# Sixteen copies of the bias lines read eight times, the identity's load on another queue, and a third pair of banks in the mixer's projections

## The chip, the cores and the metric

The kernel runs on one core of one Trainium2 chip. The metric is device time in microseconds (us) of one whole execution, the median of several runs. One core has TensorE (PE, matmuls, with its weight loads listed apart as PEld), VectorE (DVE), ScalarE (ACT), GpSimd (POOL) and SyncE (SP), which here only starts transfers; DMA queues move data between the device memory and the core's memory.

## The reference, cut to what matters

Two layers of a decoder trunk on an input of 256 tokens by 1024 channels:

```python
for l in range(2):
    x = x + 0.5 * swiglu(rms_norm(x, norm_gain[l, 0]), w_ffn_in[l, 0], w_ffn_out[l, 0])
    x = x + hybrid_mixer(rms_norm(x, norm_gain[l, 1]), w_in[l], ..., rel_bias)
    x = x + 0.5 * swiglu(rms_norm(x, norm_gain[l, 2]), w_ffn_in[l, 1], w_ffn_out[l, 1])
```

`swiglu` multiplies by a 1024 x 5632 matrix, gates, and multiplies by a 2816 x 1024 matrix. `hybrid_mixer` has one wide input projection (8420 columns) whose columns feed four attention branches (A: top-64 selection, B: one block of 256 keys, C: low-rank latents with rotary keys, D: three dilated windows) and four sigmoid gates; the branches are projected, gated, summed and projected once more. Branches A, B and D add a bias that depends on the distance between query and key, from one table `rel_bias` that both layers share:

```python
bias = bias_table[:, rel_bucket(dist)]          # 20 heads, 32 buckets
logits = einsum(q, k) * scale + bias
```

## The kernel before

Activations stay on the chip. Weights stream once from device memory, 237 MB in all, through five buffers of 1 MB (`raw`), filled in order by the queue of SP; a load waits until its buffer is free. Every product of 32-bit numbers is made from two parts of each factor: `split` (L172) lets ACT cast a weight to its high part `whi` (L187) and DVE (sometimes POOL) subtract to get the low part `wlo` (L188); `mm3` (L191) then runs three matmuls, `mm2` (L196) two with the weights held still. So PE needs three things for a piece of weight: the transfer, the cast, the subtraction.

The program is a chain of six blocks, FFN, mixer and FFN in each layer. `ffn` (L223) loops j from 0 to 10 over 256 columns of the gate and the value half (`up`) and, one step behind, over two rows of 128 of the output matrix (`down`). In the first FFN the loop calls `setup` once, at j = 3 (L356). `setup` (L403) loads the small tables through ACT's queue, and makes the bias: a 21 x 384 table of lines (20 heads and the mask) is built by one matmul, sent to device memory (`ld`, L421), copied there 128 times (`rep`, 4032 KB, L426) and read back skewed by one element per partition, so that partition p holds the distances of query p (`bias`, 2688 KB, L428). The order of DMAs inside `setup` is fixed. All three go through SP's queue, among the weights.

`mixer` (L469) computes ten projections of the normalised input, one after the other: column starts 804, 0, 384, 1316, 1700, 1988, 2500, 3012, 3524 and 4036. Each takes a pair of PSUM banks from `tiles` (L478): banks a2 and a3 in one turn, the double bank a01 in the next. Between them come the uses of a projection: `head_rsqrt` (square on ACT L461, sum on DVE L463, mean L111, power on POOL L114, product L116), the scaled heads `zn` on DVE (L544, L640), and their transposes by matmuls with the identity on PE (L531). The scores of branch B (`sl`, L829, softmax steps L576, L587 and L589) use the banks of a01; the low-rank products (`cqs`, `cks`, L764) and the gates (L884) use the two buffers of the pool pm.

What sets the order: a scheduler simulates the program and orders each engine's instructions by readiness, so that a change of banks or of a DMA's place moves instructions on all engines. Where two strands are joined by hand, the order of PE, ACT and DVE is pinned.

At the start, x is loaded by SP, `ident` (the 128 x 128 identity, L94) by POOL's queue, `rows` (the gains, L100) by ACT's queue; the first PE instruction (L102) transposes `rows` with `ident`, then x is transposed (L132), scaled by DVE (`xg`, L135) and split (`h`, L136 on ACT, L139 on DVE).

Of the kernel before, what the change touches and what calls it, by code (L numbers as in the profile page):

```python
# [9 lines left out]
F32 = mybir.dt.float32  # L10
# [7 lines left out]
T = 256  # L18
NT = 2
# [11 lines left out]
NLINE = 21  # L31
LLEN = 384
# [36 lines left out]
def tile_trunk(ctx: ExitStack, tc: tile.TileContext, a: dict, out: bass.AP):  # L69
    nc = tc.nc  # L70
# [8 lines left out]
    dr = ctx.enter_context(tc.tile_pool(name="dr", bufs=1, space=bass.MemoryType.DRAM))  # L79
    pa = ctx.enter_context(tc.tile_pool(name="pa", bufs=1, space=PSUM))  # L80
    pm = ctx.enter_context(tc.tile_pool(name="pm", bufs=2, space=PSUM))
# [9 lines left out]

    load_x(0)
    ident = const.tile([128, 128], F32, name="ident")
    nc.gpsimd.dma_start(out=ident[:], in_=a["ident"])  # L94

    ones = const.tile([128, 128], F32, name="ones")
    nc.vector.memset(ones[:], 1.0)
# [64 lines left out]
    def raw_tile(name="raw"):  # L162
        return raw_p.tile([128, 2048], F32, name=name, tag="raw")
# [59 lines left out]
    def ffn(l, s, nxt=None, aside=None):  # L223
# [10 lines left out]
        def load_up(j):  # L234
            rv = []
            for g in range(2):
                rv.append(raw_tile()[:].rearrange("p (k n) -> p k n", k=KC))
                c0 = g * DFF + j * 256
                if early:
                    for q in range(2):  # L240
                        nc.sync.dma_start(out=rv[g][:, 4 * q:4 * q + 4], in_=wi[:, 4 * q:4 * q + 4, c0:c0 + 256])
                        if j == g == q == 0:
                            load_x(1)
                else:
                    nc.sync.dma_start(out=rv[g], in_=wi[:, :, c0:c0 + 256])
            return rv
# [10 lines left out]
        def up_first(j, w):  # L257

            for c in range(2):
                act[2 * j + c] = pair_tile()  # L260
            for i in range(NT):
                t = slice(i * 128, (i + 1) * 128)
                ps = pm.tile([128, 2, T], F32, name="pm", tag="pm")
                for g in range(2):
                    for k in range(KC):
                        wh, wl = w[2 * g + k // 4]
                        mm3(ps[:, g, :], hh[:, k, t], hl[:, k, t], wh[:, k % 4, :], wl[:, k % 4, :],
                            k == 0, k == KC - 1)
                    if i == 0:
                        yield  # L270
                sl = wk.tile([128, T], F32, name="sl", tag="sl")
                nc.scalar.activation(out=sl[:], in_=ps[:, 0, :], func=AF.Silu, scale=rs[:, i:i + 1])
                av = wk.tile([128, T], F32, name="av", tag="av")
                nc.vector.scalar_tensor_tensor(out=av[:], in0=ps[:, 1, :], scalar=rs[:, i:i + 1], in1=sl[:],
                                               op0=ALU.mult, op1=ALU.mult)
                if j == i == 0:
                    while todo:
                        todo.pop(0)()
                pst = pt.tile([128, 4, 128], F32, name="pt", tag="pt")
                for c in range(2):  # L280
                    nc.tensor.transpose(pst[:, c, :], av[:, c * 128:(c + 1) * 128], ident[:])
                for c in range(2):
                    ah, al = act[2 * j + c]
                    nc.scalar.copy(ah[:, t], pst[:, c, :])
                    nc.vector.tensor_tensor(al[:, t], pst[:, c, :], f(ah[:, t]), op=ALU.subtract)
# [64 lines left out]
        for j in range(1, NFF // 2):  # L350
            if j < 2:
                for _ in up_first(j, w1):
                    pass
            else:
                up(j, load_up(j))
            if aside and j == 3:  # L356
                aside()
            for m in ((2 * j - 4, 2 * j - 3) if j > 1 else ()):
                w = down_w(m)
                for i in range(NT):  # L360
                    down(m, w, i)
# [36 lines left out]
    bias = const.tile([128, NLINE, T], F32, name="bias")  # L398
# [3 lines left out]

    def setup():  # L403

        oh = wk.tile([32, LLEN], F32, name="oh", tag="xn")
        tc.keep_in_program_order(nc.scalar.dma_start(out=oh[:], in_=a["onehot"]))
        rb = wk.tile([32, 32], F32, name="rb", tag="sl")
        nc.vector.memset(rb[:], 0.0)
        tc.keep_in_program_order(nc.scalar.dma_start(out=rb[0:20, :], in_=a["rel_bias"]))
        dm = wk.tile([NLINE, LLEN], F32, name="dm", tag="e", bufs=3)  # L410
        tc.keep_in_program_order(nc.scalar.dma_start(out=dm[:], in_=a["dmask"]))
        ps = pt.tile([128, 512], F32, name="pt", tag="pt")
        nc.tensor.transpose(ps[:32, :32], rb[:], ident[:32, :32])
        rbt = wk.tile([32, 32], F32, name="rbt", tag="av")
        nc.vector.tensor_copy(rbt[:], ps[:32, :32])
        ps = pt.tile([128, 512], F32, name="pt", tag="pt")
        nc.tensor.matmul(ps[:NLINE, :LLEN], lhsT=rbt[:, :NLINE], rhs=oh[:], start=True, stop=True)
        line = wk.tile([NLINE, LLEN], F32, name="line", tag="e", bufs=3)
        nc.vector.tensor_tensor(line[:], ps[:NLINE, :LLEN], dm[:], op=ALU.add)
        ld = dr.tile([NLINE, LLEN], F32, name="ld")  # L420
        tc.keep_in_program_order(nc.sync.dma_start(out=ld[:], in_=line[:]))  # L421
        rep = dr.tile([NLINE, 128, LLEN], F32, name="rep")
        rv = rep[:]
        lv = ld[:]
        src = bass.AP(tensor=lv.tensor, offset=lv.offset, ap=[[LLEN, NLINE], [0, 128], [1, LLEN]])
        tc.keep_in_program_order(nc.sync.dma_start(out=rep[:], in_=src))  # L426
        src = bass.AP(tensor=rv.tensor, offset=rv.offset + 127, ap=[[LLEN - 1, 128], [128 * LLEN, NLINE], [1, T]])
        tc.keep_in_program_order(nc.sync.dma_start(out=bias[:], in_=src))  # L428

        def load(dst, src):  # L430
            tc.keep_in_program_order(nc.scalar.dma_start(out=dst, in_=src))

        for i in range(NT):
            load(rope[:, i, :], a["rope"][i * 128:(i + 1) * 128, :])
        for qk in range(2):
            for l in range(DEPTH):
                load(gc[:, qk, l, :], a["qk_gain_c"][l, qk:qk + 1, :].partition_broadcast(128))
        gr = wk.tile([96, 128], F32, name="gr", tag="sl")
        nc.vector.memset(gr[64:96, :], 0.0)
        load(gr[0:64, :], a["b_gate"].rearrange("l n (c p) -> (l n c) p", p=128))  # L440
        for j, nm in enumerate(("qk_gain_a", "qk_gain_b", "qk_gain_d")):
            for e in range(2):
                load(gr[64 + 4 * j:68 + 4 * j, 64 * e:64 * e + 64], a[nm].rearrange("l q c -> (l q) c"))
        load(gr[76:82, :], a["mla_norm_q"].rearrange("l (c p) -> (l c) p", p=128))
        load(gr[82:86, :], a["mla_norm_kv"].rearrange("l (c p) -> (l c) p", p=128))
        ps = pt.tile([128, 512], F32, name="pt", tag="pt")
        nc.tensor.transpose(ps[:, :96], gr[:], ident[:96, :96])
        nc.vector.tensor_copy(gT[:], ps[:, :96])
        nc.vector.tensor_scalar(out=gT[:, 0:64], in0=gT[:, 0:64], scalar1=0.5, scalar2=None, op0=ALU.mult)
        for j in range(3):  # L450
            for l in range(DEPTH):
                c = 64 + 4 * j + 2 * l
                nc.vector.tensor_scalar(out=gT[:, c:c + 1], in0=gT[:, c:c + 1], scalar1=0.125, scalar2=None,
                                        op0=ALU.mult)
        nc.vector.tensor_scalar(out=gc[:, 0], in0=gc[:, 0], scalar1=96.0 ** -0.5, scalar2=None, op0=ALU.mult)

    def head_rsqrt(v, nh, w, by=None):

# [10 lines left out]
    def mixer(l, nxt):  # L469
        wi = a["w_in"][l].rearrange("(k p) n -> p k n", p=128)  # L470

        turn = [0]
# [4 lines left out]

        def tiles():  # L478
            turn[0] += 1
            if turn[0] % 2:  # L480
                return [pa.tile([128, 512], F32, name="zp", tag=f"a{2 + i}")[:] for i in range(NT)]
            z = pa.tile([128, 2, 512], F32, name="zp", tag="a01")
            return [z[:, 0, :], z[:, 1, :]]
# [477 lines left out]
        for h in range(2):  # L961
            for q in range(2):
                rv = raw_tile()[:].rearrange("p (k n) -> p k n", k=4)
# [19 lines left out]
    blocks = []  # L983
    for l in reversed(range(DEPTH)):
        blocks.insert(0, ffn(l, 1, (blocks[0], l + 1, 0) if blocks else None))
        blocks.insert(0, mixer(l, (blocks[0], l, 2)))
        blocks.insert(0, ffn(l, 0, (blocks[0], l, 1), None if l else setup))
    main, stats, h = norm(0, 0)
    todo = next(blocks[0])
    main(0)  # L990
# [43 lines left out]
```

## Time and profile before

| what | value |
|---|---|
| median of 3 runs | 1386.67 us (1386.07 to 1387.12) |
| profiled execution | 1388.2 us, of which the profile's span is 1386.4 us |
| PE busy, share of the span | 1351.8 us, 98% |
| DVE, ACT, POOL busy | 951.3, 687.5, 337.3 us |
| HBM read | 234.51 MB, 173 GB/s over the span |
| rep, bias | 4032 KB and 2688 KB |

Busy times of different engines overlap. Idle time of PE is the span less its busy time; the granted clock is the TensorE clock as a share of its full 2.4 GHz. Stretches are given in us from the span's start. The two layers run the same code at different times (the mixer's projections lie at about 230 to 320 us in the first and 915 to 1000 us in the second).

### The profile page before, as it was taken

To read this page: it belongs to the slowest core of one execution; us is meant where nothing else is said; L and a number is where in the kernel's file an instruction comes from. 1 tells how busy PE (TensorE), PEld (TensorE's weight loads), DVE (VectorE), ACT (ScalarE), POOL (GpSimd) and SP (SyncE) were. 2 spreads that over 40 slices of the span, in tenths; PEclk is the share of its full clock that TensorE was granted. 3 is DMA by queue.
4 is the path that set the end of the run, shared out by engine and by line. 5 is a ranking of instruction groups with operands and counts; after the bars stand their busy time and mean duration, and the time that the engine had idled before them with its cause. 6 is when DMAs were issued, how large, how long until landed. Compare 5 with 4: busy or idle time off the path is not lost.

```text
span 1386.4 us, 21269 instructions
## 1 busy us (share of the span) xinstructions
PE 1351.8 (98%) x8241; PEld 1195.4 (86%) x8241; DVE 951.3 (69%) x1642; ACT 687.5 (50%) x1052; POOL 337.3 (24%) x281
## 2 busy tenths in 40 slices
PE   7998999999999999999999999999999999999998
PEld 7887889879988989888898888898789989888887
DVE  6747756777587686666577766567865976776663
ACT  6425444655454556444454444355554455554441
POOL 0212342140022041322502232323300412222231
PEclk9999999999999999999999999999999999999999
DMA  9549733545343365655556555354543424665530
GB/s 356 168 165 371 246 119 118 184 150 185 114 136 117 122 203 193 209 185 183 182 167 198 182 183 197 96 170 155 180 140 122 153 92 136 210 209 196 193 122 31
DMA packets 173589, 236.96 MB, mean 171 GB/s; under 512 B 5085, under 2 KB 144545, under 8 KB 173489
## 3 DMA queue, kind: packets, MB, share of 16 engines
q1 hardware_dynamic: 172275, 235.16, 51.3%
q8 instruction: 65, 1.06, 0.3%
q10 hardware_dynamic: 1182, 0.38, 0.1%
q14 instruction: 35, 0.29, 0.1%
q0 software_dynamic: 32, 0.07, 0.0%
HBM read 234.51 MB, written 5.21 MB: 173 GB/s over the span
## 4 chain that ended last, share of the span: by engine, by line
PE 90%; DVE 5%; ACT 2%; issue 1%; DMA 1%; POOL 1%; SPq 0%; ACTq 0%; DVEq 0%; POOLq 0%
PE pt L199 9%; PE pm L199 9%; PE pm L192 7%; PE pm L194 7%; PE pm L193 7%; PE acc L192 6%; PE acc L193 6%; PE acc L194 6%; PE pt L200 5%; PE pm L200 5%; PE zp L193 4%; PE zp L194 4%; PE zp L192 4%; PE ov L604 2%; DVE wlo L188 2%
## 5 line engine op out<-in xcount | busy, mean ns | idle before, releaser
L187 ACT CAST whi<-raw 128x1024 fp32r<-128x1024 f32 (+5 forms) x446 | 452.3, 1020 | 416.6 <-PE pm L193 96.9
L188 DVE TENSOR_TENSOR wlo<-raw,whi 128x1024 fp32r<-128x1024 f32 (+3 forms) x426 | 514.3, 1212 | 167.7 <-ACT whi L187 165.4
L199 PE MATMUL pt<-h,whi 128*128 128x512 f32 x576 | 210.5, 399 | 2.9 <-ACT whi L187 2.9
L199 PE MATMUL pm<-h,whi 128*128 128x512 f32 x576 | 208.5, 396 | 0.0
L308 POOL TENSOR_TENSOR sl<-sl,rb 128x256 f32<-128x256 f32 x72 | 82.9, 1151 | 326.1 <-ACT sl L307 324.6
L200 PE MATMUL pt<-h,wlo 128*128 128x256 f32 x576 | 150.5, 282 | 0.8 <-DVE wlo L188 0.8
L200 PE MATMUL pm<-h,wlo 128*128 128x256 f32 x576 | 149.6, 280 | 0.0
L192 PE MATMUL pm<-h,whi 128*128 128x256 f32 x512 | 148.0, 289 | 1.3 <-DVE tg L922 1.3
L194 PE MATMUL pm<-h,wlo 128*128 128x256 f32 x512 | 147.1, 287 | 0.0
L193 PE MATMUL pm<-h,whi 128*128 128x256 f32 x512 | 146.8, 287 | 0.0
L193 PE MATMUL acc<-wlo,act 128*128 128x512 f32 x352 | 138.4, 393 | 0.0
L194 PE MATMUL acc<-whi,act 128*128 128x512 f32 x352 | 138.0, 392 | 0.0
L192 PE MATMUL acc<-whi,act 128*128 128x512 f32 x352 | 137.9, 393 | 0.0
L199 PEld LDWEIGHTS pt<-h,whi 128*128 128x128 f32 x576 | 109.0, 189 | 22.9 <-ACT whi L187 3.2
L199 PEld LDWEIGHTS pm<-h,whi 128*128 128x128 f32 x576 | 108.2, 188 | 20.8 <-issue 0.6
L312 POOL TENSOR_TENSOR act<-av,act 128x256 fp32r<-128x256 f32 x72 | 83.4, 1159 | 165.3 <-ACT act L311 157.5
L193 PE MATMUL zp<-wlo,h 128*128 128x512 f32 (+4 forms) x320 | 115.9, 363 | 1.1 <-DVE wlo L188 1.1
L200 PEld LDWEIGHTS pt<-h,wlo 128*128 128x128 f32 x576 | 109.4, 190 | 7.3 <-DVE wlo L188 1.1
L194 PE MATMUL zp<-whi,h 128*128 128x512 f32 (+4 forms) x320 | 114.4, 358 | 0.0
L200 PEld LDWEIGHTS pm<-h,wlo 128*128 128x128 f32 x576 | 108.7, 189 | 6.4
L192 PE MATMUL zp<-whi,h 128*128 128x512 f32 (+4 forms) x320 | 110.1, 361 | 1.2 <-ACT whi L187 1.2
L192 PEld LDWEIGHTS pm<-h,whi 128*128 128x128 f32 x512 | 97.7, 191 | 5.3 <-issue 4.3
(200 smaller groups left out, 2485.6 us busy)
## 6 DMA issues: line engine op xcount, KB each, us to landing
raw<-in_w_ffn_in_dram SPq DMA_DIRECT2D x66, 1024.0 KB
raw<-in_w_in_dram SPq DMA_DIRECT2D x52, 1024.0 KB
raw<-in_w_ffn_out_dram SPq DMA_DIRECT2D x44, 1024.0 KB
raw<-in_w_ffn_in_dram SPq DMA_DIRECT2D x44, 512.0 KB
raw<-in_w_branch_dram SPq DMA_DIRECT2D x8, 1024.0 KB
raw<-in_w_out_dram SPq DMA_DIRECT2D x8, 1024.0 KB
raw<-in_w_in_dram SPq DMA_DIRECT2D x8, 768.0 KB
rep<-ld SPq DMA_DIRECT2D x1, 4032.0 KB
```

The costliest lines, as they stand in the source:

```text
L187: nc.scalar.copy(hv, src)
L188: (eng or nc.vector).tensor_tensor(lv, src, f(hv), op=ALU.subtract)
L192: nc.tensor.matmul(ps, lhsT=lh, rhs=rh, start=start, stop=False)
L193: nc.tensor.matmul(ps, lhsT=lh, rhs=rl, start=False, stop=False)
L194: nc.tensor.matmul(ps, lhsT=ll, rhs=rh, start=False, stop=stop)
L199: parts = [lambda: nc.tensor.matmul(ps, lhsT=wh, rhs=r2, start=start, stop=stop), lambda: nc.tensor.matmul(ps[:, 0], lhsT=wl, rhs=r2[:, 0] ...
L200: lambda: nc.tensor.matmul(ps[:, 0], lhsT=wl, rhs=r2[:, 0], start=False, stop=False)]
L308: nc.gpsimd.tensor_tensor(sl[:], sl[:], rb[:], op=ALU.mult)
L312: nc.gpsimd.tensor_tensor(al, av[:], f(ah), op=ALU.subtract)
L604: nc.tensor.matmul(o[:, h, :], lhsT=pT[:, j, :], rhs=pv(j), start=j == 0, stop=j == nb - 1)
```

## The change

Three edits.

- The bias: `rep` holds 16 copies of the whole table of lines (16 x 8064 elements, 504 KB) instead of 128 copies of each line, and `bias` is filled by eight reads of 16 partitions (336 KB each) instead of one of 128. `setup` is a generator that is advanced once in each step of the FFN's loop: at j = 3 everything but the copies and reads, at j = 4 the copies, at j = 5 to 8 two reads each.
- `ident` is loaded by ACT's queue, ahead of `rows`.
- `tiles` of the mixer takes its banks in three turns: the two buffers of pm, the double bank a01, banks a2 and a3.

```diff
-    nc.gpsimd.dma_start(out=ident[:], in_=a["ident"])
+    nc.scalar.dma_start(out=ident[:], in_=a["ident"])
...
-            if aside and j == 3:
-                aside()
+            if aside and j > 2:
+                next(aside, None)
...
-        rep = dr.tile([NLINE, 128, LLEN], F32, name="rep")
-        rv = rep[:]
-        lv = ld[:]
-        src = bass.AP(tensor=lv.tensor, offset=lv.offset, ap=[[LLEN, NLINE], [0, 128], [1, LLEN]])
-        tc.keep_in_program_order(nc.sync.dma_start(out=rep[:], in_=src))
-        src = bass.AP(tensor=rv.tensor, offset=rv.offset + 127, ap=[[LLEN - 1, 128], [128 * LLEN, NLINE], [1, T]])
-        tc.keep_in_program_order(nc.sync.dma_start(out=bias[:], in_=src))
...
+        yield
+        rep = dr.tile([16, NLINE * LLEN], F32, name="rep")
+        lv, rv = ld[:], rep[:]
+        src = bass.AP(tensor=lv.tensor, offset=lv.offset, ap=[[0, 16], [1, NLINE * LLEN]])
+        tc.keep_in_program_order(nc.sync.dma_start(out=rv, in_=src))
+        for b in range(8):
+            if b % 2 == 0:
+                yield
+            src = bass.AP(tensor=rv.tensor, offset=rv.offset + 127 - 16 * b,
+                          ap=[[NLINE * LLEN - 1, 16], [LLEN, NLINE], [1, T]])
+            tc.keep_in_program_order(nc.sync.dma_start(out=bias[16 * b:16 * b + 16], in_=src))
...
-            if turn[0] % 2:
+            if turn[0] % 3 == 1:
+                return [pm.tile([128, 512], F32, name="zp", tag="pm")[:] for i in range(NT)]
+            if turn[0] % 3 == 0:
                 return [pa.tile([128, 512], F32, name="zp", tag=f"a{2 + i}")[:] for i in range(NT)]
             z = pa.tile([128, 2, 512], F32, name="zp", tag="a01")
             return [z[:, 0, :], z[:, 1, :]]
...
-        blocks.insert(0, ffn(l, 0, (blocks[0], l, 1), None if l else setup))
+        blocks.insert(0, ffn(l, 0, (blocks[0], l, 1), None if l else setup()))
```

Lines behind the edits of `setup` stand about eight lines further down in the changed kernel (L531 is L539 there, L589 is L597, L762 is L770).

SP's queue in the first FFN, where `setup` puts its transfers among the weights (`raw` from L241 are halves of `up` weights, those from L329 `down` weights), as a piece of the difference:

```order
-L421 DMA ld<-line 21x384
-L426 DMA rep<-ld 2688x1x384
+L423 DMA ld<-line 21x384
+L455 DMA rep<-ld 16x8064
 L241 DMA raw<-in_w_ffn_in_dram 128x4x256 x2
-L329 DMA raw<-in_w_ffn_out_dram 128x2x1024
-L241 DMA raw<-in_w_ffn_in_dram 128x4x256 x2
-L428 DMA bias<-rep 128x21x256
-L241 DMA raw<-in_w_ffn_in_dram 128x4x256 x2
+L461 DMA bias<-rep 16x21x256 x4
 L329 DMA raw<-in_w_ffn_out_dram 128x2x1024
```

The copies keep their place behind `ld`; four of the eight reads come directly behind the next two weight loads, the other four further down.

PE in the first mixer, at the end of branch B (`ov` is probabilities times values, `pt<-ident,bo` transposes branch B's output, `pm<-br` multiplies it with its output weights, `pm<-h_1926` or `pm<-h_1933` are the gates). Before:

```order
L194 MATMUL pm<-h_1926,wlo 128x256
L604 MATMUL ov<-bv,pT 128x65 x2
L618 MATMUL pt<-ident,bo 128x128 x2
L597 MATMUL pt<-ident,e 128x128
L604 MATMUL ov<-cv,pT 128x65
```

After, in the same place:

```order
L194 MATMUL pm<-h_1933,wlo 128x256
L626 MATMUL pt<-ident,bo 128x128 x2
L605 MATMUL pt<-ident,e 128x128
L612 MATMUL ov<-cv,pT 128x65
L605 MATMUL pt<-ident,e 128x128
L192 MATMUL pm<-br,whi 128x256 x2
L612 MATMUL ov<-cv,pT 128x65
```

The two products `ov<-bv` (L612) have moved forward: 21 matmuls `pm<-h_1933` now stand between them and the transposes of `bo` (L626).

ACT in the first mixer, during the projection from column 4036, whose weights are cast in pieces of 128 x 512 (`cq`, `ck` are branch C's transposed heads, `e` the exponentials of the scores). Before:

```order
L762 COPY cq<-pt 96x4x128
L187 CAST whi<-raw 128x512
L762 COPY ck<-pt 96x4x128
L187 CAST whi<-raw 128x512
L187 CAST whi<-raw 128x1024 x2
```

After:

```order
L770 COPY cq<-pt 96x4x128
L187 CAST whi<-raw 128x512
L597 ACT_TABLE_LOAD
L597 ACTIVATE e<-e,nm 128x128 x4
L187 CAST whi<-raw 128x512
L770 COPY ck<-pt 96x4x128
L187 CAST whi<-raw 128x512
L187 CAST whi<-raw 128x1024
```

The table load and four exponentials of branch B, which before stand behind all casts of the projections, now stand ahead of the last two casts of 128 x 512; on DVE the softmax steps L576 and L587 move with them.

## Rows read from the trace of the kernel before

**Rows 1.** The page: busy time by engine; the chain that ended last.

```profile
PE 1351.8 (98%) x8241; PEld 1195.4 (86%) x8241; DVE 951.3 (69%) x1642; ACT 687.5 (50%) x1052; POOL 337.3 (24%) x281
PE 90%; DVE 5%; ACT 2%; issue 1%; DMA 1%; POOL 1%; SPq 0%; ACTq 0%; DVEq 0%; POOLq 0%
```

**Rows 2.** PE's waits, by line: line <- releaser: us in total, times, longest.

```profile
PE pt L531 <- DVE zn L544: 3.3, 4, 1.2
PE pt L618 <- DVE bo L611: 2.1, 2, 1.0
PE ov L604 <- DVE pT L601: 1.4, 2, 0.7
PE pt L531 <- DVE zn L640: 1.2, 2, 0.6
```

**Rows 3.** Timeline of SP: start, duration, issue.

```profile
78.54 0.88 SPq L426 DMA_DIRECT2D rep<-ld  x1
79.59 21.38 SPq L241 DMA_DIRECT2D raw<-in_w_ffn_in_dram  x2
106.44 2.38 SPq L428 DMA_DIRECT2D bias<-rep  x1
```

**Rows 4.** Stretches: start:end, length, busy of PE, PEld, DVE, ACT, POOL, clock, DMA share, GB/s.

```profile
80.00:98.00 18.00, 18.00 (x102) 15.59 (x101) 12.05 (x24) 5.31 (x8) 3.58 (x4) 1.00 0.45 163
106.00:112.00 6.00, 2.32 (x12) 1.56 (x11) 1.47 (x2) 2.54 (x3) 0.00 (x0) 1.00 1.02 364
112.00:118.00 6.00, 6.00 (x26) 5.18 (x26) 6.00 (x7) 3.90 (x6) 3.25 (x2) 0.72 1.09 365
```

**Rows 5.** Timelines of ACT and PE at 109 us; idle time before and its releaser in brackets.

```profile
109.46 3.89 ACT L187 CAST whi<-raw 128x1024 fp32r<-128x1024 f32 x4 [14.47 <-DMA raw<-in_w_ffn_in_dram]
110.56 0.50 PE L199 MATMUL pt<-h,whi 128*128 128x512 f32 x1 [2.93 <-ACT whi L187]
```

**Rows 6.** The start: the chain's piece of `ident`; timelines of PE and ACT.

```profile
1.25 4.72 DMA ident<-in_ident_dram
...
6.01 0.34 PE L102 MATMUL pt<-ident,rows 48*128 48x48 f32 x1 [6.01 <-DMA ident<-in_ident_dram]
...
4.38 0.63 ACT L145 ACTIVATE junk<-x 128x512 f32<-128x512 f32 x1 [1.89 <-DMA x<-in_x_dram]
```

**Rows 7.** Timelines of PE at two transposes of the first mixer, and PE's pace.

```profile
237.51 0.41 PE L531 MATMUL pt<-ident,zn 128*128 128x128 f32 x2 [0.62 <-DVE zn L640]
...
237.94 0.34 PE L193 MATMUL zp<-wlo,h 128*128 128x384 f32 x1
238.11 0.34 PE L194 MATMUL zp<-whi,h 128*128 128x384 f32 x1
...
277.56 0.66 PE L531 MATMUL pt<-ident,zn 128*128 128x128 f32 x4 [0.46 <-DVE zn L544]
```

**Rows 8.** Stretches of the first mixer: the low-rank part, the last projections, branch B's end.

```profile
290.00:300.00 10.00, 6.84 (x34) 4.94 (x33) 7.37 (x16) 6.58 (x11) 5.70 (x4) 1.00 0.41 136
300.00:320.00 20.00, 20.00 (x123) 17.75 (x122) 19.38 (x52) 9.86 (x14) 4.67 (x5) 1.00 0.65 206
352.00:356.00 4.00, 2.25 (x15) 1.84 (x15) 3.72 (x11) 2.98 (x7) 0.11 (x1) 0.88 0.23 91
354.00:360.00 6.00, 5.45 (x35) 5.33 (x35) 2.77 (x12) 2.28 (x8) 0.00 (x0) 0.72 0.01 3
```

**Rows 9.** Groups of DVE (busy, mean ns | idle), 250 to 420; timelines of DVE, ACT.

```profile
L587 DVE TENSOR_SCALAR nm<-mx 128x1 f32<-128x1 f32 x20 | 2.0, 146 | 0.0
...
L576 DVE CUSTOM_DVE_ANT_0 e<-sl,bias 128x128 f32<-128x128 f32 x8 | 1.9, 287 | 2.1 <-PE sl L829 1.6 <-PE pt L597 0.5
...
353.08 1.22 DVE L188 TENSOR_TENSOR wlo<-raw,whi 128x1024 fp32r<-128x1024 f32 x1
...
312.94 0.62 ACT L187 CAST whi<-raw 128x512 fp32r<-128x512 f32 x1 [2.21 <-issue]
...
323.65 1.28 ACT L589 ACT_TABLE_LOAD   x1
```

## The prediction

> **What bounds the kernel now.** I read the page first. PE is busy 98% of the span and makes up 90% of the chain that ended last; DVE, the next engine, is busy 69% [rows 1]. PE does the same matmuls after the change, so what can be won is only the time in which it stands still, 1386.4 - 1351.8 = 34.6 us, and the time in which its granted clock is below 1.00. Then I read PE's waits, to see whose they are [rows 2], and the stretches in which PE is not full, to see how long each is and what the clock does behind it [rows 4, 8]. The three edits touch three such places.
>
> The largest is at 106 to 112 us, where PE is busy for 2.32 of 6 us [rows 4]. The matmul at 110.56 had waited 2.93 us for a cast on ACT, and ACT itself had stood idle for 14.47 us until a weight landed [rows 5]. SP tells why: `rep` is issued at 78.54, the next two weight loads hang in the queue from 79.59 for 21.38 us, and only then come the rest [rows 3]. While `rep` runs, 80 to 98, the DMA engines are busy 45% and move 163 GB/s; in 106 to 118 they are full at about 365 GB/s [rows 4]. So for some 20 us the weights stand behind a transfer that uses less than half of the engines. PE lives on what was loaded before: the loads issued before `rep` feed it to 110.56 - 2.93 = 107.6 us [rows 5], 28 us after 79.59.
>
> **The bias: -5.4 us.** What goes if the hole closes is 6 - 2.32 = 3.7 us of waiting, and behind it the clock: 112 to 118 is granted 0.72 on the mean (some of it at the lower level, 1.2 GHz), which costs 6 x 0.28 = 1.7 us [rows 4]. Together 5.4 us. Does it close? The new `rep` is 504 KB, an eighth: at the 163 GB/s of the old one 3.1 us, at 365 GB/s 1.4 us. Behind it two weight loads of 512 KB, then four reads, 1.38 MB, then weights again. The reads have no row here. The nearest ones bound them: 3.8 us at 365 GB/s, 8.4 us at 163 GB/s [rows 4]. So the weights behind them come at most 3.1 + 8.4 + 1.0/0.163 = 17.7 us after 79.6, with ten of the 28 us to spare; this holds over the whole bound, so I take the full 5.4. What is late next is nothing near: ACT and DVE are idle before the hole (ACT 5.31 and DVE 12.05 of 18 us busy in 80 to 98 [rows 4]), and the last four reads, with 0.69 MB each time, stand in front of weights at a time when five buffers are full again. The other steps of `setup` stay where they are.
>
> The rule that speaks against these reads stands in the Trainium skill, "SBUF — State Buffer", section "Door 1: The DMA port swizzle": partitions 0 to 15 are reached by four ports, measured there at 104 GB/s. By it the four reads take an estimated 13 us instead of 3.8 to 8.4 and the hole still closes, with about five us left; no run so far shows such a transfer. The same skill, "DMA: Bandwidth & Descriptors", section "Why a DMA increments its semaphore by 16 and not by 1", lets the slowest dimension set how many engines share a transfer, 7 for one of 21 and 16 for the new one of 16; the 45% busy share during the old `rep` (7 of 16 is 44%) agrees with it.
>
> **The identity: -0.2 us.** PE's first instruction waits 6.01 us for `ident`, whose transfer takes 4.72 us from 1.25; x is there at 4.38 [rows 6]. On ACT's queue the load is issued about 0.5 us sooner and may land with x, so up to 6.0 - 4.5 = 1.5 us could go. But in the changed order DVE makes the first `wlo` (1.22 us, such as the one in [rows 9]) ahead of the scaled x, and ACT takes the second tile's statistics before it casts `h`. What PE wins at the transposes it waits for at the first product of `h`. Bounds: -1.5 (all of it) to +1.2 (the `wlo` on the path); I take -0.2, since the two nearly cancel.
>
> **Three pairs of banks: waits of projections, -2.1 us.** With two pairs in turns, PE cannot begin the next-but-one projection until the uses of this one are over, so the transposes at L531 stand between projections with little work in front. At 237.51 and 277.56 they wait 0.62 and 0.46 us [rows 7]; in both layers that makes the 1.2 of the second L531 row and 0.9 out of the 3.3 of the first [rows 2]. In the changed order of PE there are 23 matmuls of the next projection ahead of them, at 0.17 us each (237.94 to 238.11) some 4 us [rows 7], far over both waits. I take all, 2.1.
>
> **The low-rank part, -0.5 us.** In 290 to 300 PE is idle 3.16 us, POOL's power on eight heads among the causes [rows 8]. In the changed order the same low-rank matmuls stand ahead of the same transposes, so most of it stays: 0 to -1 us per layer, -0.25 each.
>
> **Branch B's end, -0.6 and -1.7 us.** PE waits for `bo` (2.1 us in two waits) and `pT` (1.4 in two) [rows 2]; at 352 to 356 it is busy 2.25 of 4 us and the clock in 354 to 360 is 0.72, another 6 x 0.28 = 1.7 us [rows 8]. The 21 gate matmuls that now stand ahead of L618 take 2.5 us and cover `bo`. But DVE's order now has a `wlo` of 1.22 us [rows 9] ahead of the step that makes `br` for the next products, of which PE's own work there covers some 0.3: about 0.9 us come back, and about 0.5 of the `pT` wait stays. 1.75 becomes 1.4 or 1.5 per layer, -0.3 each, -0.6 in all. Whether the clock falls is open. After 1.75 us of idle time within 4 us it fell; with 3.16 us spread over ten (290 to 300) it stayed at 1.00 [rows 8]. The new waits lie between those two rows, so I take half of the two dips (2 x 1.7), -1.7, and keep 0 and -3.4.
>
> **What moves into the last projections, +1.0 us.** Branch B's scores and softmax steps now lie inside 300 to 320, where DVE is already busy 19.38 of 20 us [rows 8]. DVE gets four L576 of 0.29 us, two of twice the elements, at most 0.57 each, and six L587 of 0.15 [rows 9]: 3.2 us. ACT gets the table load, 1.28, and four exponentials, each at most the 0.62 of a cast with four times the elements [rows 9]: 3.8 us against 2.21 idle just before that cast. On the other side PE gets the score matmuls there too, which gives both engines time. From below the cost is 0 or a gain (the same steps no longer stand behind the projections), from above all 7.0 us per layer. Each excess alone, about 1.5 us on ACT, is met by slack of a like size, so I take 0.5 per layer, 1.0 in all.
>
> **The sum.** -5.4 - 0.2 - 2.1 - 0.5 - 0.6 - 1.7 + 1.0 = -9.5 us. The profiled execution took 1388.2 us with its span of 1386.4, and would take 1378.7; it lies 1.5 us over the median of the runs, 1386.67. For the median: **1377.2 us**.
>
> **The rivals.** (A) Branch B's end is cleared whole: the gate matmuls cover every wait (2.9 us more), the clock never falls there (1.7 more), and nothing stalls in 300 to 320 (1.0). For it: there are 2.5 us of new cover; against it: the `wlo` ahead of `br`. 1371.6 us.
> (B) The hole stays, so that the bias edit does nothing. One engine of the old `rep` moved 163/7 = 23 GB/s (an estimate, if seven of 16 worked, as 45% says). If a read of 16 partitions runs on one or two engines, the four take 30 to 60 us and the weights miss the 28. Against it: the old read of 128 partitions ran in a stretch at 365 GB/s with the weights. 1382.6 us.
> (C) **Slower.** DVE and ACT become the bound at 300 to 320 and 980 to 1000: L587 waits for scores, the exponentials for L587, the cast behind them for the exponentials, its `wlo` for the cast, PE for that. If nothing overlaps it costs 7.0 us a layer, 14 in all in place of the 1.0: 1390.2 us. It decides from 5.3 us of new PE idle time in each layer there (10.5 over two layers eats all gains). For it: 19.38 of 20 us; against it: DVE's list there has steps that nobody waits for soon.
> (D) The identity gives its whole 1.5 us: 1375.9 us.
>
> **How the numbers follow.** Forecast 0.60, A 0.13, B 0.10, C 0.10, D 0.07. What a measurement can tell from no change here is about 0.2%, 2.8 us: below 1383.9 is faster, above 1389.4 slower. Forecast with its bounds, A, D and two thirds of B lie below, with about 0.05 of the forecast's own spread taken off for dips that stay, start at its worst and stalls of a few us: faster 0.82. The rest of B, that 0.05 and a part of C make 0.11 for the same, C's remainder 0.07 for slower. The range goes from 1370.5 (A with a little of the low-rank part) to 1385.0 (B with a slow start), which leaves out most of C and the case that A, D and the low-rank part come together, about 0.18.
>
> **What would show it.** Right: no PE wait for `whi` near 107 us and a clock of 1.00 in 112 to 118; weights issued soon after `rep`, DMA share well over 0.45 there; no waits at L539 after the second and fifth projections; 300 to 320 with PE idle under 1 us. Wrong: a hole that only moved, to where the last four reads stand; PE idle for over 3 us in the last projections; the dip at branch B's end unchanged in both layers, which costs 1.7 of the sum; a first `h` product no earlier, or later, than 10 us.

## The result and the profile after

The changed kernel takes **1378.35 us** (1377.51 to 1378.57, 4 runs), the kernel before 1386.89 us (1386.07 to 1387.39, 4 runs); the ratio is 0.9937 with an interval of 0.9924 to 0.9949. That is 8.5 us faster, where 9.5 were forecast. Some parts of the forecast hit and some missed, and the misses to either side nearly cancel, so part of the closeness is luck.

First the page of the changed kernel, busy time by engine and the chain, as in [rows 1].

```profile
span 1376.7 us, 21253 instructions
PE 1349.9 (98%) x8241; PEld 1193.8 (87%) x8241; DVE 951.8 (69%) x1642; ACT 689.4 (50%) x1052; POOL 334.7 (24%) x280
PE 92%; DVE 4%; ACT 2%; issue 1%; POOL 1%; DMA 0%; SPq 0%; ACTq 0%; DVEq 0%
```

PE's idle time went from 34.6 to 26.8 us, its busy time down by 1.9. Next the stretches that answer to [rows 4, 8]; columns as there.

```profile
88.00:98.00 10.00, 10.00 (x59) 8.73 (x58) 8.48 (x11) 5.30 (x8) 3.18 (x3) 1.00 1.16 117
106.00:112.00 6.00, 6.00 (x36) 5.21 (x35) 5.23 (x7) 3.73 (x6) 2.68 (x2) 1.00 1.17 155
112.00:118.00 6.00, 6.00 (x35) 5.22 (x34) 4.72 (x7) 2.61 (x4) 2.35 (x2) 1.00 1.02 339
290.00:300.00 10.00, 8.83 (x44) 6.88 (x43) 9.18 (x22) 5.74 (x9) 6.14 (x5) 1.00 0.46 148
300.00:320.00 20.00, 20.00 (x129) 17.16 (x129) 17.94 (x59) 12.13 (x21) 1.01 (x1) 1.00 0.50 160
344.00:350.00 6.00, 4.89 (x40) 4.45 (x39) 4.53 (x10) 3.63 (x8) 0.11 (x1) 1.00 0.40 123
350.00:356.00 6.00, 6.00 (x51) 5.56 (x50) 3.89 (x11) 2.22 (x4) 0.00 (x0) 1.00 0.14 57
```

The hole at 106 to 112 is gone, and so is the low clock behind it. The last projections (300 to 320) have no PE idle time. Branch B's end (344 to 350) waits 1.11 us where [rows 8] show 1.75, and the clock behind it stays at 1.00. PE's waits, to hold against [rows 2]:

```profile
PE pt L102 <- DMA rows<-in_norm_gain_dram: 5.8, 1, 5.8
PE pt L539 <- DVE zn L552: 2.4, 2, 1.2
PE ov L612 <- DVE pT L609: 1.3, 2, 0.7
PE ov L612 <- ACT pT L607: 0.9, 2, 0.5
```

The waits for the second `zn` row and for `bo` are no longer there, and of the first `zn` row only the two of the low-rank part are left. The first instruction now waits for `rows`.

A table made from the start times of the same PE instruction in both traces tells where the 9.6 us of the two profiled executions lie. Each row's difference holds all that came before it.

| PE instruction | before, us | after, us | difference |
|---|---|---|---|
| transpose of `rel_bias`, L413 (L415), first FFN | 71.72 | 73.10 | +1.38 |
| first `zp` product of the first mixer | 206.04 | 201.75 | -4.29 |
| first `pt<-ik,aqk`, behind branch B, first mixer | 378.40 | 371.60 | -6.80 |
| first `zp` product of the second mixer | 888.46 | 881.55 | -6.91 |
| first `pt<-ik,aqk` of the second mixer | 1061.03 | 1051.47 | -9.56 |
| last `acc` product | 1382.18 | 1372.62 | -9.56 |

So the start lost 1.4, the hole gave 5.7, each mixer gave 2.5 to 2.65, and all of it by the end of branch B. Two things stick out. The start is longer, not shorter. And the first mixer gave only 2.5 although its waits and low clock, added up (0.62, 0.46, 0.3, 0.64 and 1.7), had gone by 3.7.

### The profile page after: what moved, and what is told of

Same layout as the page of the kernel before. It is cut to its first block, busy times and chain, and to the rows that moved or that the text cites. A ratio compares the mean times of both kernels' runs of the same rounds, so it can differ in the third digit from the quotient of the medians.

```text
span 1376.7 us, 21253 instructions
## 1 busy us (share of the span) xinstructions
PE 1349.9 (98%) x8241; PEld 1193.8 (87%) x8241; DVE 951.8 (69%) x1642; ACT 689.4 (50%) x1052; POOL 334.7 (24%) x280
## 4 chain that ended last, share of the span: by engine, by line
PE 92%; DVE 4%; ACT 2%; issue 1%; POOL 1%; DMA 0%; SPq 0%; ACTq 0%; DVEq 0%
PE pt L199 10%; PE pm L199 10%; PE pm L192 7%; PE pm L194 7%; PE pm L193 7%; PE acc L193 6%; PE acc L192 6%; PE acc L194 6%; PE pt L200 5%; PE pm L200 5%; PE zp L193 4%; PE zp L194 4%; PE zp L192 4%; PE ov L612 2%; DVE wlo L188 1%; PE sl L837 1%
```

## The experiments

Theory after this reading: the three edits act apart, the identity's move costs because it changes an order, and the scores of branch B that moved forward steady the clock but make PE's own steps dearer. The rivals are written in the expectations.

### Each edit alone, and the change without the identity's move

`e1` is the kernel before with only this:

```diff
-    nc.gpsimd.dma_start(out=ident[:], in_=a["ident"])
+    nc.scalar.dma_start(out=ident[:], in_=a["ident"])
```

> The kernel before with only the identity's load on ScalarE's queue, ahead of the gains. Theory (from where the two traces drift apart): the start got 1.4 us longer, because the changed order puts the second tile's statistics, whose x lands at 7.85 us, ahead of the second weight's cast; so 1386.9 + 1.4 = 1388.3 us. Rival (the prediction's term): the earlier issue is worth 0.2 us, up to 1.5; 1386.7 to 1385.4 us, and the 1.4 us of the trace belongs to something else.

`e2` has only the bias edit (`setup` and its calls), `e3` only the three lines of `tiles`.

> The kernel before with only the sixteen copies, the eight reads and their places in the loop. Theory: the hole at 107 us and the low clock behind it go, 5.4 to 5.7 us: 1381.2 to 1381.5 us, PE's order elsewhere as before. Rival: the hole closed only because the changed start delays the demand for weights by 1.4 us; then PE waits for weights again near 107 us, 1383 us or more.

> The kernel before with only the three pairs of banks in the mixer. Theory: each mixer wins 2.5 us (3.75 us of idle and low-clock time less some 1.2 us that the scattered scores add to PE's own steps): 1381.8 us, no drop of the clock at branch B's end in either layer. Rival: the clock holds at branch B's end only because everything before it moved; then the drops of 1.7 us stay in this kernel, 1385 us.

`e4` is the changed kernel with the first diff undone.

> The changed kernel with the identity back on GpSimd's queue. Theory: the three edits add up, and this leaves out the one that costs: 1378.35 - 1.4 = 1377.0 us. Rival: the identity's move wins its 0.2 us and the rest of the kernel pays for something else: 1378.5 us or a little more.

| kernel | median, us | ratio to before (95%) | mean granted clock | mean of span x clock, us |
|---|---|---|---|---|
| before (17 executions beside these) | 1387.36 | 1 | 0.9964 | 1380.7 |
| e1, identity | 1388.68 | 1.0007 (0.9997 to 1.0017) | 0.9966 | 1381.6 |
| e2, bias | 1382.48 | 0.9964 (0.9952 to 0.9976) | 0.9974 | 1376.9 |
| e3, banks | 1381.97 | 0.9962 (0.9949 to 0.9974) | 0.9990 | 1379.0 |
| e4, bias and banks | 1377.24 | 0.9930 (0.9918 to 0.9942) | 0.9998 | 1375.4 |
| after, all three | 1378.35 | 0.9937 (0.9924 to 0.9949) | 1.0000 | 1376.3 |

The medians of e2 and e3 add up: 4.9 + 5.4 = 10.3, and e4 wins 10.1. So e3 and e4 came within 0.3 us of what was expected, and e2 1.0 us above it. The last column, the span times its granted clock, is a measure worked out here for the time without the low clock. It is an estimate: the clock is on record to three decimals, which is 0.7 us of the span of one execution either way, and a low clock costs less than it counts where PE waits. It splits the win of e4: 5.3 us are waits (3.8 of the bias, 1.7 of the banks, which is 5.5) and the rest is clock.

The kernel before draws its clock anew in each execution: of 60 executions beside the experiments 6 had 1.000 with spans of 1382.3 to 1382.9 us, and 8 had 0.995 with 1386.7 to 1387.8. Each drop that comes costs up to 1.7 us, and the same wait may bring it or not. In e2 branch B's end waits 1.75 us in both layers (the last window below begins inside the first of two waits and shows 1.50 of it), with no drop in the first layer and with one in the second:

```profile
106.00:112.00 6.00, 6.00 (x36) 5.21 (x35) 4.12 (x6) 2.98 (x4) 2.20 (x2) 1.00 1.14 117
112.00:118.00 6.00, 6.00 (x33) 5.16 (x32) 5.27 (x8) 2.82 (x4) 2.90 (x3) 1.00 1.03 360
344.00:352.00 8.00, 6.25 (x46) 5.66 (x46) 5.68 (x20) 4.12 (x10) 0.11 (x1) 1.00 0.39 129
1028.00:1036.00 8.00, 6.50 (x44) 6.20 (x44) 4.76 (x15) 4.27 (x11) 0.00 (x0) 0.79 0.04 17
```

The profiled executions give a count. Where branch B's end waits 1.75 us (before, e1, e2 and, below, e5, e6 and e9, two layers each) the clock fell behind it in 6 of 12 places; where it waits 1.1 us or less (after, e3, e4, e7, e8, e10, e11 and e12) in none of 16. So in e3 too it holds with nothing but the banks changed, against the rival of e3. Behind the hole it fell each time that there was one (before, e1, e3 and e7).

The first two lines above also refute the rival of e2: the hole closes without the changed start. By the start times of the same instructions e2 is 0.02 us behind the kernel before until the hole and 5.65 ahead after it.

e1 alone lies inside its interval around no change, so its time does not decide. Its trace does: the first product with `wlo` is 0.75 us later than before, and the same matmul 0.85 later at 24 us and 0.90 at the end. In the column without the low clock it costs 0.9, and so does the step from e4 to after (1375.4 to 1376.3). The start of the changed kernel shows the mechanism, PE, DVE and ACT by start and duration:

```profile
5.84 0.31 PE L102 MATMUL pt<-ident,rows 48*128 48x48 f32 x1 [5.84 <-DMA rows<-in_norm_gain_dram]
8.85 1.97 PE L132 MATMUL pt<-ident,x 128*128 128x128 f32 x8 [0.79 <-DVE xg L135]
10.84 0.58 PE L192 MATMUL pm<-whi,h 128*128 128x256 f32 x1
12.18 0.58 PE L194 MATMUL pm<-whi,h 128*128 128x256 f32 x1 [0.55 <-DVE h L139]
...
6.96 1.23 DVE L188 TENSOR_TENSOR wlo<-raw,whi 128x1024 fp32r<-128x1024 f32 x1 [0.56 <-ACT whi L187]
8.11 1.28 DVE L135 TENSOR_TENSOR xg<-pt,gn 128x512 f32<-128x512 f32 x2
10.29 1.23 DVE L188 TENSOR_TENSOR wlo<-raw,whi 128x1024 fp32r<-128x1024 f32 x1 [0.84 <-ACT whi L187]
11.44 1.29 DVE L139 TENSOR_TENSOR h<-xg,h 128x512 fp32r<-128x512 f32 x2
...
7.87 0.63 ACT L145 ACTIVATE junk<-x 128x512 f32<-128x512 f32 x1 [0.93 <-DMA x<-in_x_dram]
9.22 1.04 ACT L187 CAST whi<-raw 128x1024 fp32r<-128x1024 f32 x1
```

Before, PE transposed both tiles of x without a wait, and the first product started at 9.80:

```profile
6.28 3.87 PE L132 MATMUL pt<-ident,x 128*128 128x128 f32 x16
9.80 0.56 PE L192 MATMUL pm<-whi,h 128*128 128x256 f32 x1
```

With the identity ahead on the same queue, `rows` became the last to land, and PE's first instruction came only 0.17 us sooner (6.01 in [rows 6]). The rest is the changed order. DVE makes the first `wlo` (6.96) ahead of `xg` (8.11), so PE waits 0.79 us for `xg` at the second half of its transposes, and the first product comes at 10.84, straight behind them. On ACT the second tile's statistics stand ahead of the second cast. That tile lands at 7.8 us, ACT stands for it, and the cast comes at 9.22; DVE makes its `wlo` (10.29) ahead of `h` (11.44), for which PE waits 0.55 us at 12.18. e1 shows the same two waits, 0.83 and 0.49 us. PE's products behind them begin 0.21 us apart (12.98, 13.19) where before they begin 0.12 apart (11.11, 11.23); the clock column shows 1.00 for both, so the reason for this pace stays open. The kernel before loses 0.92 us to two later waits that the changed one does not have, and at 24 us the difference is 1.4.

### Is it the transfer or the order?

`e8` issues the identity from SP's queue right behind x, so that VectorE keeps the old order.

```diff
-    nc.scalar.dma_start(out=ident[:], in_=a["ident"])
+    nc.sync.dma_start(out=ident[:], in_=a["ident"])
```

> The changed kernel with the identity issued by the queue of SP, right behind the first tile of x. Theory: what costs at the start is the order on ScalarE and VectorE (the second tile's statistics and the first low part ahead of the scaled x), not the transfer; this kernel's VectorE keeps the old order, so the start is as before or up to 0.5 us sooner: 1377.0 us. Rival: the first PE instruction waits for whichever of the small transfers lands last in a full DMA; then it still starts at 5.8 to 6.2 us and the time is 1377.2 us to 1378.3 us according to ScalarE's order.

It took 1376.97 us (1376.73 to 1377.30), 0.9931 (0.9918 to 0.9943). PE and ACT at its start:

```profile
4.54 0.31 PE L102 MATMUL pt<-ident,rows 48*128 48x48 f32 x1 [4.54 <-DMA ident<-in_ident_dram]
9.23 1.94 PE L132 MATMUL pt<-ident,x 128*128 128x128 f32 x8 [2.48 <-DMA x<-in_x_dram]
10.82 0.56 PE L192 MATMUL pm<-whi,h 128*128 128x256 f32 x1
...
7.81 1.04 ACT L187 CAST whi<-raw 128x1024 fp32r<-128x1024 f32 x1 [2.21 <-DMA raw<-in_w_ffn_in_dram]
```

PE's first instruction comes 1.47 us sooner, and nothing is won: the second tile of x, for which PE now waits 2.48 us, lands at 9.2 us and the first weight at 7.8, both later than before, and at 24 us PE is where it was before (0.02 us later). The rival's guess of 5.8 to 6.2 us for the first instruction was wrong, and so was the hope of up to 0.5. In these traces the start is bound by the loads of x and of the weights and by the casts and subtractions behind them, not by the identity.

### The hole: engines, bytes or the number of reads

`e6` keeps 128 copies and one read of 128 partitions, and only turns the copy's layout.

```diff
-        rep = dr.tile([NLINE, 128, LLEN], F32, name="rep")
+        rep = dr.tile([128, NLINE * LLEN], F32, name="rep")
...
-        src = bass.AP(tensor=lv.tensor, offset=lv.offset, ap=[[LLEN, NLINE], [0, 128], [1, LLEN]])
+        src = bass.AP(tensor=lv.tensor, offset=lv.offset, ap=[[0, 128], [1, NLINE * LLEN]])
...
-        src = bass.AP(tensor=rv.tensor, offset=rv.offset + 127, ap=[[LLEN - 1, 128], [128 * LLEN, NLINE], [1, T]])
+        src = bass.AP(tensor=rv.tensor, offset=rv.offset + 127, ap=[[NLINE * LLEN - 1, 128], [LLEN, NLINE], [1, T]])
```

> The kernel before with 128 copies of the whole table (128 x 8064 elements) in place of 128 copies of each line, and one read of 128 partitions as before; nothing else. Bytes and number of transfers are those of before, only the slowest dimension of the copy is 128 and not 21. Theory: the copy ran on 7 of 16 engines; now it runs at 300 GB/s or more, takes some 12 us and not 24, and the hole closes as with the sixteen copies: 1382.3 us, with no clock loss at 112. Rival: a copy within the device memory is slow in itself; then it takes over 20 us, the hole stays and the time is 1387 us.

1381.71 us, 0.9963 (0.9952 to 0.9975), the same as e2. While the copy runs and where the hole was:

```profile
80.00:90.00 10.00, 10.00 (x56) 8.59 (x55) 7.78 (x17) 3.58 (x5) 0.74 (x1) 1.00 1.08 347
106.00:112.00 6.00, 6.00 (x36) 5.25 (x35) 5.34 (x8) 1.78 (x3) 1.88 (x2) 1.00 1.10 365
```

The same 4032 KB go at 347 GB/s with all engines busy, where before they went at 163 with a share of 0.45 [rows 4]. The new layout also copies longer contiguous pieces than the 384 elements of a line, but that is not what made the difference: a busy engine moves 163 / (16 x 0.45) = 23 GB/s before and 347 / (16 x 1.08) = 20 in e6, so it is the number of engines that grew. So the hole was made by the layout with its slowest dimension of 21, not by the bytes. The Trainium skill, "DMA: Bandwidth & Descriptors", section "Why a DMA increments its semaphore by 16 and not by 1", takes as many engines as the largest number up to 16 that divides the slowest dimensions: 7 for 21 and 16 for 128. The shares of 0.45 (7 of 16 is 0.44) and 1.08 agree.

`e7` puts all eight reads in one row (the `yield` of every second read only ahead of the first).

```diff
-            if b % 2 == 0:
+            if b == 0:
                 yield
```

> The kernel of the run without the identity's move, with all eight reads in one row behind the copies. Theory: a read into 16 partitions runs at 105 to 120 GB/s, whatever the engines could do (in the changed kernel 86.5 to 98 us show 106 to 121 GB/s with engines shown busy), so eight of them hold the queue for 24 us instead of 12; the weights behind land at about 111 us, PE waits some 1 to 4 us there, and the time is 1378 to 1382 us. Rival: the low rate belongs to the mixture of four reads with weight loads, and eight in a row run faster; then no wait and 1377.2 us.

1385.88 us (1384.08 to 1386.97), 0.9995 (0.9986 to 1.0004), 8.6 us more than e4 and far beyond the 1 to 4 us expected. Stretches of e7, and then the timeline of ACT:

```profile
86.00:106.00 20.00, 20.00 (x108) 17.12 (x107) 11.01 (x15) 6.12 (x9) 4.87 (x4) 1.00 1.14 113
112.00:120.00 8.00, 1.54 (x10) 1.08 (x8) 3.79 (x6) 4.69 (x6) 2.18 (x2) 0.92 1.07 395
120.00:126.00 6.00, 5.83 (x19) 5.01 (x20) 5.34 (x8) 2.71 (x4) 2.35 (x2) 0.53 0.94 323
```

```profile
113.42 1.04 ACT L187 CAST whi<-raw 128x1024 fp32r<-128x1024 f32 x1 [16.82 <-DMA raw<-in_w_ffn_out_dram]
```

A read into 16 partitions moves 113 GB/s while the engines are shown busy, for the whole 20 us. ACT stands for 16.82 us until a weight lands, PE is idle for 6.5 us and then runs at a low clock. The Trainium skill, "SBUF — State Buffer", section "Door 1: The DMA port swizzle", has 104 GB/s for partitions 0 to 15, and this trace agrees within a tenth, for reads that go to all eight groups of 16. So the eight reads together (2688 KB, some 24 us at 113 GB/s) are as slow as the copy that they replaced (4032 KB at 163 GB/s, some 25 us), and what saves the change is that they are spread: four, two and two, with weights between.

### What the third pair does

`e5` takes the three pairs in another turn (a01, pm, a2 and a3), so that the last projection holds a01 and the scores stay late; `e11` takes a2 and a3, a01, pm.

> The kernel of the run without the identity's move, with the three pairs of banks taken in another turn (a01, pm, a2 and a3), so that the last projection holds a01 and branch B's scores stay behind the projections as before. Theory: the waits at the two transposes go with any third pair (2.1 us), but what steadies the clock at branch B's end, and what makes PE's own steps 1.2 us a layer dearer, are the scores that move ahead; so here no PE wait after the second and fifth projections, branch B's end waits 1.75 us a layer as before, the mean granted clock falls to about 0.998, and the median is 1378.5 to 1379.5 us. Rival: the third pair alone steadies the clock; then it stays at 1.000 with 1376 us or less, since the scattered scores cost nothing here.

> The kernel of the run without the identity's move, with the turns a2 and a3, a01, pm: again no projection holds pm next to the low-rank part, and a01 is free from the eighth projection on, so the scores move forward as in the change. Theory: what matters is which pair is held beside the low-rank part (in the turn that lost, pm was) and when a01 comes free; this one wins as the change does: 1376.5 to 1378 us, waits at L539 only in the low-rank part, clock 1.000. Rival: any turn but the change's loses, since pm is also taken by the ninth projection, just ahead of the gates: 1380 us or more.

Both lost: 1389.38 us, 1.0017 (1.0008 to 1.0025), and 1391.88 us, 1.0044 (1.0027 to 1.0060). PE at the low-rank part and the stretch behind it, in e5 and then in e11:

```profile
287.88 0.66 PE L539 MATMUL pt<-ident,zn 128*128 128x128 f32 x2 [4.51 <-DVE zn L552]
...
288.00:294.00 6.00, 4.79 (x18) 4.32 (x19) 1.85 (x4) 1.41 (x3) 2.38 (x3) 0.50 0.22 78
```

```profile
295.04 1.09 PE L539 MATMUL pt<-ident,zn 128*128 128x128 f32 x4 [4.45 <-DVE zn L552]
...
295.00:301.00 6.00, 5.96 (x24) 4.67 (x25) 4.32 (x18) 1.51 (x2) 1.22 (x2) 0.50 0.55 176
```

e5 gives pm to the eighth projection (3012), e11 to the ninth (3524). Between these two lies the low-rank part, which needs pm for its own results. In e5 it cannot begin until the eighth projection has been read out of pm (its first product comes at 290.49, behind the wait, against 283.77 in the changed kernel); in e11 the ninth projection cannot begin until the low-rank results have been read (301.25 against 292.56). So nothing covers PE while the chain for `zn` runs: it waits 4.5 us in each layer beside the wait of 1.2 that all these kernels have, and behind this the clock is at its lower level, 0.50 for 6 us. The mean clock is 0.9935 in e5 and 0.9920 in e11, so a large part of the loss is clock. Which bank holds what is read here from the code and the order; no run frees pm alone. Neither run could answer its question about the scores; e11's rival was right in its number.

`e9` keeps the change's first nine turns and gives only the last projection a01.

```diff
-            if turn[0] % 3 == 1:
+            if turn[0] % 3 == 1 and turn[0] < 10:
```

> The kernel of the run without the identity's move, but the last projection (column 4036) takes the double bank a01 and not pm; the first nine turns are those of the change, so PE's order is the same up to the scores, which stay behind the projections. Theory: the third pair wins the two transposes' waits (2.1 us), and the scores' move wins 0.65 us of waits a layer at branch B's end and the clock there, and costs about 0.6 us a layer in PE's own steps; so here branch B's end waits 1.75 us a layer, the clock falls there in some of the executions (mean 0.998 to 0.999), and the median is 1378.5 to 1380 us. Rival: the third pair alone does it all; then 1377.2 us or less and a clock of 1.000.

1377.98 us (1376.58 to 1378.85), 0.9939 (0.9926 to 0.9952) with a mean clock of 0.9984 over its five executions and a span x clock of 1374.0. Branch B's end in e9, then in e4:

```profile
344.00:350.00 6.00, 4.25 (x35) 3.81 (x34) 5.00 (x20) 3.88 (x9) 0.11 (x1) 1.00 0.34 137
```

```profile
344.00:350.00 6.00, 4.89 (x40) 4.45 (x39) 4.70 (x13) 3.26 (x9) 0.00 (x0) 1.00 0.55 176
```

With late scores PE waits 0.64 us more there, and still goes from the first `zp` product to the first `pt<-ik,aqk` in 169.40 us (200.69 to 370.09), against 169.84 in e4 (200.66 to 370.50). The other waits between these two points are the same in both traces, so the order with the moved scores costs PE 0.64 + 0.44 = 1.1 us a layer in steps of its own. The after trace shows such a step, two score matmuls alone among projections; the before trace shows eight in a row:

```profile
301.63 0.63 PE L192 MATMUL zp<-whi,h 128*128 128x512 f32 x2
302.18 0.49 PE L837 MATMUL sl<-bqk 64*128 64x128 f32 x2
302.60 0.50 PE L193 MATMUL zp<-wlo,h 128*128 128x512 f32 x1
```

```profile
323.67 0.72 PE L829 MATMUL sl<-bqk 64*128 64x128 f32 x8
324.31 0.39 PE L192 MATMUL pm<-h,whi 128*128 128x256 f32 x1
```

Two take 0.42 us until the next begins, eight take 0.64. By start times the sixteen score matmuls of a layer account for 0.4 of the 1.1 us (2.74 us in e4, 2.33 in e9), and the projections' own matmuls, among which they stand, for 0.6; why these take longer no run shows. The theory's mechanism held, but its time for e9 was too high by half a us or more: in the column without the low clock e9 is 1.4 us faster than e4, and its lower clock takes that back and a little more (the medians, 0.7 us apart, can't be told apart by their intervals). That the moved scores steady the clock rests on five executions each (0.9998 against 0.9984) and on the count of drops above.

### Putting parts together

`e10` has the layout of e6 and the three pairs, `e12` also the identity behind x.

> The kernel before with the 128 copies of the whole table and the three pairs of banks, the identity on GpSimd's queue: no sixteen copies, no eight reads, no places in the loop. Theory: a closed hole is worth the same however it is closed, so this is as fast as the changed kernel without the identity's move: 1377.2 us, within 0.7. Rival: the 5.7 MB more that it moves are felt somewhere, or the weights behind a 4 MB copy come late for one step: 1379 us or more.

> The kernel before with the 128 copies of the whole table, the three pairs of banks as in the change, and the identity behind the first tile of x on SP's queue. Theory: each of the three closes its place and no more is to be had there; the start is bound by the loads and by ScalarE's and VectorE's order, so this is within 0.5 us of the kernels that have two of the three: 1376.5 to 1377.3 us, clock 1.000. Rival: the identity's earlier arrival (PE's first instruction 1.5 us sooner) is worth its 1.5 us here: 1375.8 us or less.

1377.31 us, 0.9932 (0.9920 to 0.9944), and 1377.60 us, 0.9939 (0.9925 to 0.9952). As the theory says, a closed hole is worth the same however it is closed; e10 moves 3.6 MB more than e4 (not the 5.7 of its expectation) and is no slower. e12 lies 0.3 us over the range of its theory, and far from its rival. e8, e4 and e10 have medians 1.0 to 1.4 us under the changed kernel's, but by the intervals of their ratios none of these kernels can be told apart from the changed one or from another.

## Why the prediction held, step by step

- **The bias, -5.4: right in size, by a wrong bound.** The profile gives 5.65. In the median it is 4.9 (e2): the low clock behind the hole, 1.7 of the 5.4, doesn't come in each execution (6 of 60 before had a clock of 1.000 throughout). The bound on the four reads, 3.8 to 8.4 us, was wrong: they run at 117 GB/s (88 to 98 above), some 12 us. No row of the kernel before showed a transfer into few partitions, so neither of the two rates in [rows 4] was an end of the range. The estimate beside it by the Trainium skill, 13 us, came near. The "ten us to spare" were fewer: in e7 four reads more, some 12 us, bring 6.5 us of PE idle time, so about 5.5 were left. That the hole closed all the same was margin, not the bound.
- **The identity, -0.2: wrong.** It costs about 0.9 by the column without the low clock (0.75 to 1.4 in the traces). The step that failed is "what PE wins at the transposes it waits for at the first product": PE won 0.17 us at its first instruction, since `rows`, one place behind on the same queue, became the last to land, and lost 0.79 within the transposes, since the `wlo` ahead of `xg` was on the path. The second tile's statistics, which the prediction names without a price, cost a further wait of 0.55. The bound of +1.2, "the `wlo` on the path", came near, and so did the sign of being wrong: the first product came at 10.84 us, later than 10.
- **The two transposes, -2.1: right.** Both waits are gone in both layers, under 23 matmuls as counted.
- **The low-rank part, -0.5: right.** 3.16 us became 2.8 in each layer, -0.7 in all.
- **Branch B's end, -0.6 and -1.7: both too small.** Of 1.75 us a layer 1.1 stay, -1.3 in all, and the clock dropped in none of the four executions of the changed kernel. Taking half of the drops was a coin's choice between two rows. With the old wait of 1.75 us it is one in fact (6 of 12 places), with the new one of 1.1 no drop was seen.
- **The last projections, +1.0: the size was about half, the cause another.** DVE and ACT made PE wait for nothing there (20.00 of 20 us), so a right sign here was luck. What was not in the sum at all is that PE itself pays for the order with score matmuls strewn among projections, 1.1 us a layer, 2.2 in all.

Between the two profiled executions the win is 9.6 us, as forecast, and the terms as they came out add up to it: -5.7 + 1.4 - 2.2 - 0.7 - 1.3 - 3.4 + 2.2 = -9.7, 0.1 from the table. The mechanisms were right for most of it, but the sum was close by luck: the identity (1.1 us worse than forecast in the median, 1.6 in the profile) and the strewn scores (1.2 worse than the stalls that stood for them) are made up by branch B's end, better by 0.7 in waits and by 1.7 in clock, and by half a us of the hole and the low-rank part. That 9.6 is 8.5 in the medians is a step of its own: the terms were read from one execution and taken off the median, and the profiled execution of before lies 1.3 us over its median, that of the changed kernel 0.2.

Of the rivals, (A) had the clock right. (B) did not come: the reads are slow, at a third of 365 GB/s, but with a DMA share of 1.16 and not on one or two engines. (C) did not come here, and neither did (D), as the identity's earlier issue won 0.17 us at the first instruction. But e5 and e11 end where (C) ended, at 1389 to 1392 us, through a bank and not through DVE: no rival named which pair the low-rank part holds, and that decides the sign of this edit.

## What to carry to other kernels

A slow transfer ahead of the weights costs only when the stock behind it runs out, so compare its time with that stock, by its own shape: in these runs the outermost dimension of a copy and the number of partitions of a read set their rates apart from the bytes. A further buffer in a rotation helps or hurts by who else holds it in the same moment; count its other users place by place before choosing the turn. And an earlier transfer that lets a scheduler reorder the start is worth nothing if the last to land is another one.

## What the runs showed of the hardware

- The granted clock behind a wait of the same length falls in one execution and not in the next: spans of the kernel before run from 1382.3 us at a mean clock of 1.000 to 1387.8 at 0.995. Behind waits of 1.75 us in all it fell in 6 of 12 places, behind 1.1 us in none of those seen at the same spot. A single profile tells the price of a drop, not how often it comes.
- A transfer into 16 partitions moved 113 to 117 GB/s with the DMA engines shown busy at a share of 1.14 to 1.16; a copy with a share of 0.45 (7 of 16 engines would be 0.44) moved 163 GB/s. A busy share of 1 is no sign of a full rate.
- Two score matmuls set alone among matmuls of another shape took PE 0.42 us until the next began, and eight in a row 0.64.
